# A diffusion trunk layer: modulation vectors by split products, first tiles transposed earlier, the first unit's side steps later

## The chip, the cores and the metric

One core of one Trainium2 chip. The metric is the device time of one execution in microseconds (us), as the median of several executions of the same program. Times inside the program come from one profiled execution and are counted from its first instruction.

## What is computed

One layer of a trunk for 2048 latent tokens and 256 context tokens of width 1024: a bidirectional gated linear recurrence, then a gated feed-forward block. Both are preceded by a normalisation that is shifted and scaled by vectors made from `c` (latent) and `c_ctx` (context). Cut to what this change touches:

```python
sc_lat, sc_ctx = silu(c), silu(c_ctx)
m_l = (sc_lat @ w_ada[l] + b_ada[l])[:, None, :]      # w_ada: 1024 x 6144
m_c = sc_ctx @ w_ada[l] + b_ada[l]
sh1, sc1, g1, sh2, sc2, g2 = split(m_l, 6)
csh1, csc1, ... = split(m_c, 6)
hl = modulate(rmsnorm(lat, norm_g[l, 0]), sh1, sc1)   # h * (1 + scale) + shift
hc = modulate(rmsnorm(cx, norm_g[l, 0]), csh1, csc1)
yc, yl = hgrn2_mixer(hc, hl, hg_w_in[j], ...)          # first step: [hc; hl] @ hg_w_in
lat = lat + g1 * yl
lat = lat + g2 * conv_ffn(modulate(rmsnorm(lat, norm_g[l, 1]), sh2, sc2), ...)
return rmsnorm(lat, final_g)
```

## The kernel before, in words

All data is float32. Large products are done on TensorE (PE) as "split products": a matrix is cut into a high part, rounded by ScalarE (ACT) to the short format fp32r (`split`, L80), and a low part, the rest, which VectorE (DVE) computes by a subtraction (L81). Three fp32r products (high by high, low by high, high by low) then stand for one float32 product (`mm3`, L356 to L358). A product of operands in plain float32 goes through PE as two recorded instructions.

The program opens with the block of L186 to L252. It must produce the first two of the six modulation vectors, shift and scale, for both kinds of token. `w_ada`'s first 2048 columns come in as 16 tiles of 128 x 1024 (512 KB), two for each of eight blocks k of rows. The tile with i = 0 is issued from ACT's queue, that with i = 1 from SyncE's (SP). PE multiplies each as plain float32 with a stationary operand of two columns, silu(c) and silu(c_ctx) (L209), into four accumulators `mps`. ACT copies the four out (L216), 16 small transposes turn them into columns (`mt`, L220), and DVE adds `b_ada` and `norm_g` (L223 to L225): A1 is the scale, B1 the shift.

The tokens are worked in tiles of 128 and units of three tiles (384 columns): the first unit is the two context tiles and one latent tile, the second unit the next three latent tiles. The first three tiles are fetched between the `w_ada` tiles and normalised (`early_x`: ACT takes the sum of squares at L100, GpSimd (POOL) the power at L77, DVE scales at L105). Once A1 and B1 are there, each tile is transposed by PE in two groups of four blocks (`transpose_mod`, L112), modulated out of the accumulator by ACT (L116) or DVE (L119), and split into parts `hh` and `hl` (`put_split`). Then come four more tiles (`early_x(3)` to `early_x(6)`), needed from the second unit on.

The weights of head 0 (`load_feat`, `load_vg`: five tiles of `w_in`, 512 KB each) use the same 13 buffers as the `w_ada` tiles and are split too.

After that, `mixer_scan` runs eight heads by units through `unit` (L383 on). A unit begins with the two gates: two `mm3` of 24 products with 384 columns each, followed by a sigmoid on ACT (L402) and an affine step on DVE (L404). Between the products, `tick` calls side steps from the list `todo`, so that the PE never lacks work: in the first unit of all these are the six `put` steps that transpose, modulate and split the second unit's tiles. `ticks[1]` is the number of product triples over which the list is spread: 20 for a unit with context tiles (L393).

The order of instructions on each engine is not the order of the code: a scheduler of the framework sets it when the program is built, from the dependences and its own idea of durations. Each engine then works strictly through its own row, and a DMA waits for its turn in the row of the engine that issues it.

Of the kernel before, what the change touches and what calls it, by code (L numbers as in the profile page):

```python
# [9 lines left out]
F32 = mybir.dt.float32  # L10
F32R = mybir.dt.float32r
# [3 lines left out]
OP = mybir.AluOpType  # L15
# [4 lines left out]
D = 1024  # L20
# [3 lines left out]
KT = 8  # L24
# [24 lines left out]
def body(ctx, tc, a, out):  # L49
    nc = tc.nc  # L50
    pe, act, dve, pool, sp = nc.tensor, nc.scalar, nc.vector, nc.gpsimd, nc.sync
# [11 lines left out]
    ident = cst.tile([128, 128], F32, name="ident")  # L63
# [15 lines left out]
    def split(h, l, src):  # L79
        act.activation(h, src, AF.Copy)  # L80
        dve.tensor_tensor(l, src, h.bitcast(F32), OP.subtract)  # L81
# [4 lines left out]
    A1 = [small(f"A1_{i}") for i in range(2)]  # L86
    B1 = [small(f"B1_{i}") for i in range(2)]
# [16 lines left out]
        else:  # L104
            dve.tensor_scalar(xt, xt, rs, None, OP.mult)  # L105

    def transpose_mod(xt, hm, g, psp, A, B, tag, bufs, on_act):

        tp = psp.tile([128, 4, 128], F32, name="tp", tag=tag, bufs=bufs)
        for j in range(4):  # L110
            k = g * 4 + j
            pe.transpose(tp[:, j, :], xt[:, k * 128:(k + 1) * 128], ident)  # L112
        for j in range(4):
            k = g * 4 + j
            if on_act:
                act.activation(hm[:, k, :], tp[:, j, :], AF.Identity, bias=B[:, k:k + 1],  # L116
                               scale=A[:, k:k + 1])
            else:
                dve.tensor_scalar(hm[:, k, :], tp[:, j, :], A[:, k:k + 1], B[:, k:k + 1],  # L119
                                  OP.mult, OP.add)  # L120

    ch = ctx.enter_context(ExitStack())
    rawp = pool_(ch, "rawp", 2)
# [5 lines left out]
    late = Sf[:, 0:4]  # L129
# [35 lines left out]
    def load_feat(h, **kw):  # L165


        feat = []
        for ty in (2, 1):
            wh = wp.tile([128, KT, 128], F32R, name="wh", tag="wh")  # L170
            wl = wp.tile([128, KT, 128], F32R, name="wl", tag="wl")
            load_w(h, ty, wh, wl, **kw)
            feat.append((wh, wl))
        vh = wp.tile([128, KT, 384], F32R, name="vh", tag="vh", bufs=1)
        vl = wp.tile([128, KT, 384], F32R, name="vl", tag="vl", bufs=1)
        load_w(h, 0, vh[:, :, 256:], vl[:, :, 256:], **kw)
        return feat, vh, vl
# [8 lines left out]
    with ExitStack() as c0:  # L186
        p0 = pool_(c0, "p0", side="right")
        p0s = pool_(c0, "p0s", space=PSUM)
        act.activation(sil, vec[:, V_C:V_C + 16], AF.Sigmoid)
        dve.tensor_tensor(sil, sil, vec[:, V_C:V_C + 16], OP.mult)  # L190
        silv = sil.rearrange("p (two k) -> p k two", two=2)
        mps = [p0s.tile([2, 512], F32, name=f"mps{n}") for n in range(4)]
        staged = [v[:, i] for p, n in ((2, 3), (5, 3), (4, 1))
                  for v in [place(p, [128, n, D], F32, "x0")] for i in range(n)]

        def early_x(j):

            xt = x_tile(None, first[j], xt=staged[j])
            junk = p0.tile([128, D], F32, name="junk", tag="hm", bufs=3)
            normalize(xt, junk, p0)  # L200

        first = [t for u in GROUPS[0] for t in u]
        for k in range(KT):
            for i in range(2):
                wt = p0.tile([128, D], F32, name="wada", tag="wada", bufs=13)
                (sp if i else act).dma_start(
                    wt, a["w_ada"][k * 128:(k + 1) * 128, i * D:(i + 1) * D])
                for n in range(2):
                    pe.matmul(mps[2 * i + n], silv[:, k, :], wt[:, n * 512:(n + 1) * 512],  # L209
                              start=k == 0, stop=k == KT - 1)  # L210
            if 3 <= k < 6:
                early_x(k - 3)
        head0 = load_feat(0, p=p0, tag="wada", bufs=13)
        m2 = [rawp.tile([2, 2, 512], F32, name="m2", tag="raw") for _ in range(2)]
        for n in range(4):
            ada_done = act.activation(m2[n // 2][:, n % 2], mps[n], AF.Copy)  # L216
        m2f = [m.rearrange("p a b -> p (a b)") for m in m2]
        mt = p0s.tile([128, 16, 2], F32, name="mt")
        for j in range(16):
            pe.transpose(mt[:, j, :], m2f[j // 8][:, j % 8 * 128:(j % 8 + 1) * 128],  # L220
                         ident[0:2, 0:2])
        for i in (1, 0):
            dve.tensor_tensor(B1[i], mt[:, 0:8, i], vec[:, V_BA:V_BA + 8], OP.add)  # L223
            dve.tensor_tensor(A1[i], mt[:, 8:16, i], vec[:, V_BA + 8:V_BA + 16], OP.add)
            dve.scalar_tensor_tensor(A1[i], A1[i], 1.0, vec[:, V_NG:V_NG + 8], OP.add, OP.mult)  # L225
        hms = [p0.tile([128, KT, 128], F32, name="hm", tag="hm", bufs=3) for _ in range(3)]
        for g in range(2):
            ks = slice(g * 4, g * 4 + 4)
            for j, hm in enumerate(hms):
                m = 0 if first[j] >= 0 else 1  # L230
                transpose_mod(staged[j], hm, g, p0s, A1[m], B1[m], "tr", 3, (g + j) % 2)
                put_split(hm, 0, j, ks)
        with tc.issue_after(ada_done.ins):
            load_vg(0, head0, p=p0, tag="wada", bufs=13)
        for j in range(3, 7):
            early_x(j)


        l0, l1 = vec[:, V_LB:V_LB + 16], vec[:, V_LB + 16:V_LB + 32]
        mx = p0.tile([128, 16], F32, name="mx")  # L240
        e2 = p0.tile([128, 2, 16], F32, name="e2")
        eb = p0.tile([128, 32], F32, name="eb")
        pool.memset(eb, float(np.e))
        dve.tensor_tensor(mx, l0, l1, OP.max)
        dve.tensor_tensor(e2[:, 0], l0, mx, OP.subtract)
        dve.tensor_tensor(e2[:, 1], l1, mx, OP.subtract)
        e2f = e2.rearrange("p a b -> p (a b)")
        pool.tensor_tensor(e2f, eb, e2f, OP.pow)
        dve.tensor_tensor(mx, e2[:, 0], e2[:, 1], OP.add)
        dve.reciprocal(mx, mx)  # L250
        dve.tensor_tensor(lb, e2[:, 0], mx, OP.mult)
        dve.tensor_tensor(oml, e2[:, 1], mx, OP.mult)  # L252
# [26 lines left out]
    def mixer_scan():  # L279
# [82 lines left out]
        def unit(h, w, u, tiles, todo, fine=False):  # L362
# [4 lines left out]
            s0 = sum(t < 0 for t in tiles)  # L367
# [22 lines left out]

            done = [0]

            ticks = [0, 20 if s0 else 42]  # L393
            if not fine:
                tick = None

# [1 line left out]
            for d in range(2):  # L398
# [4 lines left out]
                j = (1 - d) * NH + h  # L403
# [3 lines left out]
            v = gp.tile([128, NSC, 128], F32, name="v", tag="v", bufs=2)  # L407
# [241 lines left out]
        g1s = []  # L649
        rest = ada_rest()  # L650
        todo = [f for j in range(3, 6) for f in make_h(1, j - 3, first[j], staged[j])]
        steps, fine = 0, True
        third = [make_h(2, i, t, None if i else staged[6]) for i, t in enumerate(GROUPS[0][2])]
        new = [make_h(u, i, t) for u, tiles in enumerate(GROUPS[1]) for i, t in enumerate(tiles)]
        for g, units in enumerate(GROUPS):
            for h in range(NH):
# [5 lines left out]
                for u, tiles in enumerate(units):  # L662
                    todo, fine = list(unit(h, w, u, tiles, todo, fine)), False
# [722 lines left out]
    for i, (j, cs) in enumerate(pieces):  # L1386
# [9 lines left out]
        if cs.start:  # L1396
            v = V[:, j]
# [31 lines left out]
```

## Time and profile before

| | |
|---|---|
| median of the runs before | 2866.76 us |
| lowest of the runs before | 2860.11 us |
| the profiled execution | 2865.12 us |
| its span, first to last instruction | 2863.1 us |
| PE busy in the span | 2805.9 us (98%) |
| mean granted TensorE clock | 0.994 of full speed |

How to read it: the profile lists what each engine did and what ended each idle time before an instruction. A line of the timeline gives the start and the length in us, the engine, the line of the kernel, the operation, the tile written and the tiles read, the shape, a count where equal instructions follow each other, and in brackets the idle time before it with the one that released it. Recorded lengths of instructions that follow each other on one engine overlap a little, so the price of one in a row is the distance from start to start. The granted clock is 1.00 at TensorE's upper level (2.4 GHz) and 0.50 at the lower (1.2 GHz).

### The profile page before, as it was taken

How to read it: one execution, taken by the hardware profiler on the slowest of the kernel's cores; microseconds unless marked ns; L12 is line 12 of the kernel's file. 1: busy time of each engine (PE TensorE's matmuls, PEld its weight loads, DVE VectorE, ACT ScalarE, POOL GpSimd, SP SyncE). 2: the span in 40 equal slices, each digit the busy share in tenths (PEclk: the TensorE clock that was granted, in tenths of full speed). 3: DMA queues.
4: the chain of work that ended last, by engine and by line, in shares of the span. 5: the costliest groups of instructions: out<-in, count | busy, mean ns of one | idle time of the engine just before them, and what ended most of it. 6: DMA issues, size and time to landing. Idle time of an engine off the chain costs nothing.

```text
span 2863.1 us, 43709 instructions
## 1 busy us (share of the span) xinstructions
PE 2805.9 (98%) x16016; PEld 2506.1 (88%) x16016; DVE 2110.5 (74%) x3690; ACT 1174.4 (41%) x2515; POOL 594.3 (21%) x1028
## 2 busy tenths in 40 slices
PE   7999999999999999998999799999999999999999
PEld 4999999999999999997888688888888888887887
DVE  5766666677666666577987698887888887677887
ACT  5433333365333333333555444444444444333343
POOL 2111111121111111111111353343444432000001
PEclk9999999999999999999999899999999999999999
DMA  6222222222222222135677622225522224887663
GB/s 236 69 80 77 84 79 78 78 86 81 85 90 71 84 69 87 62 94 183 266 290 276 257 88 89 82 81 176 206 88 71 77 89 136 284 298 251 196 203 122
DMA packets 202911, 386.56 MB, mean 135 GB/s; under 512 B 26692, under 2 KB 117828, under 8 KB 197448
## 3 DMA queue, kind: packets, MB, share of 16 engines
q1 hardware_dynamic: 199960, 375.51, 39.1%
q10 hardware_dynamic: 2736, 8.26, 0.8%
q8 instruction: 126, 2.06, 0.3%
q14 instruction: 89, 0.73, 0.1%
HBM read 281.70 MB, written 101.99 MB: 134 GB/s over the span
## 4 chain that ended last, share of the span: by engine, by line
PE 89%; DVE 4%; DMA 3%; ACT 2%; issue 1%; POOL 1%; SPq 0%; DVEq 0%; ACTq 0%; POOLq 0%
PE z L358 10%; PE z L356 10%; PE z L357 10%; PE y L1263 4%; PE y L1262 4%; PE y L1261 4%; PE zc L741 3%; PE zd L741 3%; PE zd L738 3%; PE zc L738 3%; PE zc L740 3%; PE zd L740 3%; PE za L741 3%; PE za L738 3%; PE za L740 3%; PE kv L574 2%
## 5 line engine op out<-in xcount | busy, mean ns | idle before, releaser
L356 PE MATMUL z<-vh,hh 128*128 128x256 f32 (+1 forms) x1024 | 300.3, 293 | 0.0
L358 PE MATMUL z<-vh,hl 128*128 128x256 f32 (+1 forms) x1024 | 293.5, 287 | 0.0
L357 PE MATMUL z<-vl,hh 128*128 128x256 f32 (+1 forms) x1024 | 293.3, 286 | 0.0
L356 PE MATMUL z<-hh,wh 128*128 128x384 f32 x768 | 264.0, 344 | 0.7 <-ACT hh L80 0.7
L357 PE MATMUL z<-hl,wh 128*128 128x384 f32 x768 | 258.5, 337 | 0.5 <-DVE hl L81 0.5
L358 PE MATMUL z<-hh,wl 128*128 128x384 f32 x768 | 258.7, 337 | 0.0
L1263 PE MATMUL y<-wd,ml 128*128 128x512 f32 x600 | 234.0, 390 | 2.3 <-DVE ml L81 2.1
L1261 PE MATMUL y<-wd,mh 128*128 128x512 f32 x600 | 233.8, 390 | 0.7 <-DVE P L1315 0.6
L1262 PE MATMUL y<-wd,mh 128*128 128x512 f32 x600 | 233.4, 389 | 0.0
L356 PEld LDWEIGHTS z<-vh,hh 128*128 128x128 f32 x1024 | 196.3, 192 | 0.0
L357 PEld LDWEIGHTS z<-vl,hh 128*128 128x128 f32 x1024 | 196.1, 191 | 0.0
L358 PEld LDWEIGHTS z<-vh,hl 128*128 128x128 f32 x1024 | 195.7, 191 | 0.0
L81 DVE TENSOR_TENSOR w<-s,w 128x512 fp32r<-128x512 f32 x132 | 145.1, 1106 | 61.6 <-ACT w L80 61.6
L484 POOL COPY TX<-S 128x3 f32<-128x3 f32 x48 | 14.6, 305 | 791.9 <-DVE S L448 791.9
L80 ACT ACTIVATE w<-raw 128x512 fp32r<-128x512 f32 x176 | 109.1, 628 | 111.6 <-DMA raw<-in_w_up_dram 43.9
L424 DVE TENSOR_TENSOR st<-z,st 128x128 f32<-128x128 f32 x127 | 36.6, 289 | 158.4 <-ACT st L423 158.2
L81 DVE TENSOR_TENSOR w<-raw,w 128x512 fp32r<-128x512 f32 x176 | 122.9, 701 | 40.4 <-ACT w L80 40.0
L1025 DVE SCALAR_TENSOR_TENSOR r<-uv,conv,r 128x1023 f32<-128x1023 f32 (+1 forms) x88 | 149.5, 1716 | 0.4
L356 PEld LDWEIGHTS z<-hh,wh 128*128 128x128 f32 x768 | 145.3, 189 | 4.4 <-DVE acc L620 1.7
L419 ACT ACTIVATE v<-z 128x128 f32<-128x128 f32 x128 | 35.5, 278 | 271.1 <-PE z L358 271.0
L357 PEld LDWEIGHTS z<-hl,wh 128*128 128x128 f32 x768 | 145.1, 189 | 0.7 <-DVE hl L81 0.7
L358 PEld LDWEIGHTS z<-hh,wl 128*128 128x128 f32 x768 | 144.8, 188 | 0.0
(325 smaller groups left out, 8172.9 us busy)
## 6 DMA issues: line engine op xcount, KB each, us to landing
raw<-in_w_up_dram SPq DMA_DIRECT2D x90, 512.0 KB, 3.9
raw<-in_w_in_dram SPq DMA_DIRECT2D x80, 512.0 KB, 3.7
lr<-m SPq DMA_DIRECT2D x49, 512.0 KB, 5.6
m<-r SPq DMA_DIRECT2D x66, 256.0 KB, 4.7
raw<-in_w_ada_dram SPq DMA_DIRECT2D x32, 512.0 KB, 4.4
stash<-st SPq DMA_DIRECT2D x125, 128.0 KB, 1.9
kq<-stash SPq DMA_DIRECT2D x15, 1024.0 KB, 7.3
og<-stash SPq DMA_DIRECT2D x15, 1024.0 KB, 6.4
```

The lines of the kernel that those rows point to most:

```text
L80: act.activation(h, src, AF.Copy)
L81: dve.tensor_tensor(l, src, h.bitcast(F32), OP.subtract)
L356: pe.matmul(o, sh[:, k], mh[:, k], start=k == 0, stop=False)
L357: pe.matmul(o, sh[:, k], ml[:, k], start=False, stop=False)
L358: pe.matmul(o, sl[:, k], mh[:, k], start=False, stop=k == KT - 1)
L738: pe.matmul(o, w[:, 0, k], r[:, :, 0, k], start=start and k == 0, stop=False, skip_group_check=True)
L740: pe.matmul(o, w[:, 0, k], r[:, :, 1, k], start=False, stop=False, skip_group_check=True)
L741: pe.matmul(o, w[:, 1, k], r[:, :, 0, k], start=False, stop=k == 3, skip_group_check=True)
L1025: dve.scalar_tensor_tensor(r, x, cw, r, OP.mult, OP.add)
L1261: pe.matmul(z, lh, rh, start=start, stop=False, skip_group_check=True)
L1262: pe.matmul(z, lh, rl, start=False, stop=False, skip_group_check=True)
L1263: pe.matmul(z, ll, rh, start=False, stop=stop, skip_group_check=True)
```

## The change

Three things, all in the opening and the first unit:

- The `w_ada` tiles are split by ACT and DVE like all other large operands, and so is the stationary operand: `s4` holds the high parts of silu(c) and silu(c_ctx) in two columns and the low parts in two more. Each tile then takes four fp32r products (high and low part, two halves of 512 columns) in place of two float32 ones. The accumulators have four rows; after the small transposes two DVE steps add the low columns to the high ones.
- The first group of transposes of the first three tiles is written ahead of the end of the `w_ada` loop (`transpose4`), and the modulation of the result stays behind it (`modulate`).
- In the first unit `ticks` starts at -8: no side step is called before the first gate's eight triples are through; the six are then spread over 20 ticks.

```diff
+        s4 = p0.tile([128, KT, 4], F32R, name="s4")
+        split(s4[:, :, 0:2], s4[:, :, 2:4], silv)
+        mps = [p0s.tile([4, 512], F32, name=f"mps{n}") for n in range(4)]
...
                 (sp if i else act).dma_start(
                     wt, a["w_ada"][k * 128:(k + 1) * 128, i * D:(i + 1) * D])
-                for n in range(2):
-                    pe.matmul(mps[2 * i + n], silv[:, k, :], wt[:, n * 512:(n + 1) * 512],
-                              start=k == 0, stop=k == KT - 1)
+                wh = rawp.tile([128, D], F32R, name="wh", tag="raw")
+                wl = p0.tile([128, D], F32R, name="wl", tag="wal", bufs=2)
+                split(wh, wl, wt)
+                for v in (wh, wl):
+                    for n in range(2):
+                        pe.matmul(mps[2 * i + n], s4[:, k], v[:, n * 512:(n + 1) * 512],
+                                  start=k == 0 and v is wh, stop=k == KT - 1 and v is wl)
             if 3 <= k < 6:
                 early_x(k - 3)
+            if k >= KT - 2:
+                for j in ((0, 1), (2,))[k - KT + 2]:
+                    tps[0, j] = transpose4(staged[j], 0, p0s, "tr", 3)
...
+        dve.tensor_copy(ml, mt4[:, :, 2:4])
+        dve.tensor_tensor(mt, mt4[:, :, 0:2], ml, OP.add)
...
-                transpose_mod(staged[j], hm, g, p0s, A1[m], B1[m], "tr", 3, (g + j) % 2)
+                if g:
+                    tps[g, j] = transpose4(staged[j], g, p0s, "tr", 3)
+                modulate(tps[g, j], hm, g, A1[m], B1[m], (g + j) % 2)
...
-            ticks = [0, 20 if s0 else 42]
+            late_ = fine == "late"
+            ticks = [-8, 20] if late_ else [0, 20 if s0 else 42]
...
-        steps, fine = 0, True
+        steps, fine = 0, "late"
```

The scheduler also moves what the diff does not name. The row of SP at the program's start, before (`x_140` and `x_143` are the first three tiles, `x_141`/`x_142` and `x_144`/`x_145` the next four, `raw` the weights of head 0):

```order
L206 DMA wada<-in_w_ada_dram 128x1024 x2
L152 DMA x_140<-in_ctx_dram 128x1024
L206 DMA wada<-in_w_ada_dram 128x1024 x2
L152 DMA x_140<-in_ctx_dram 128x1024
L206 DMA wada<-in_w_ada_dram 128x1024 x2
L152 DMA x_140<-in_x_dram 128x1024
L206 DMA wada<-in_w_ada_dram 128x1024 x2
L162 DMA raw<-in_w_in_dram 128x1024 x5
L152 DMA x_141<-in_x_dram 128x1024 x3
L152 DMA x_142<-in_x_dram 128x1024
```

The same stretch of SP's row in the changed kernel:

```order
L218 DMA wada<-in_w_ada_dram 128x1024 x2
L160 DMA x_143<-in_ctx_dram 128x1024 x2
L218 DMA wada<-in_w_ada_dram 128x1024 x2
L160 DMA x_143<-in_x_dram 128x1024
L160 DMA x_144<-in_x_dram 128x1024 x2
L218 DMA wada<-in_w_ada_dram 128x1024
L160 DMA x_144<-in_x_dram 128x1024
L160 DMA x_145<-in_x_dram 128x1024
L218 DMA wada<-in_w_ada_dram 128x1024 x3
L170 DMA raw<-in_w_in_dram 128x1024 x7
```

The four later tiles have moved from behind the weights of head 0 to a place ahead of the last three or four `w_ada` tiles of SP's row.

ACT's row where the modulation vectors are finished, before (`wh` and `vh` from `raw` are high parts of head 0's weights, `m` the copies of the accumulators, `hm` a modulated block):

```order
L100 ACTIVATE junk,ss<-x_140 128x1024
L80 ACTIVATE wh<-raw 128x1024 x2
L80 ACTIVATE vh<-raw 128x8x128
L216 ACTIVATE m_249<-mps_136 2x512
L216 ACTIVATE m_249<-mps_137 2x512
L216 ACTIVATE m_250<-mps_138 2x512
L216 ACTIVATE m_250<-mps_139 2x512
L80 ACTIVATE vh<-raw 128x8x128
L116 ACTIVATE hm<-tp,B_1_108,A_1_106 128x128 x4
```

ACT's row at the same place in the changed kernel:

```order
L80 ACTIVATE wh<-wada 128x1024 x2
L218 DMA wada<-in_w_ada_dram 128x1024
L80 ACTIVATE wh<-wada 128x1024 x3
L80 ACTIVATE wh<-raw 128x1024
L80 ACTIVATE wh<-wada 128x1024
L80 ACTIVATE wh<-raw 128x1024
L236 ACTIVATE m_363<-mps_139 4x512
L80 ACTIVATE vh<-raw 128x8x128
L236 ACTIVATE m_363<-mps_140 4x512
L236 ACTIVATE m_364<-mps_141 4x512
L236 ACTIVATE m_364<-mps_142 4x512
L80 ACTIVATE vh<-raw 128x8x128 x2
```

ACT issues its last `w_ada` tile behind the splits of the pair k = 5, and between the split of that tile and the first modulation (the row that follows, `hm` x4) stand six other splits of 128x1024 and the four copies.

DVE's row where the second unit's tiles are normalised, before (`x_141`, `x_142`: the four later tiles; `hm`: the first modulated group of the second unit; `F_430`: the first gate):

```order
L76 TENSOR_SCALAR rs<-ss 128x1 x2
L105 TENSOR_SCALAR x_141<-x_141,rs 128x1024 x2
L76 TENSOR_SCALAR rs<-ss 128x1
L105 TENSOR_SCALAR x_141<-x_141,rs 128x1024
L76 TENSOR_SCALAR rs<-ss 128x1
L105 TENSOR_SCALAR x_142<-x_142,rs 128x1024
L119 TENSOR_SCALAR hm<-tp,A_0_105,B_0_107 128x128 x4
L404 TENSOR_SCALAR F_430<-F_430,oml,lb 128x12x32
```

The same stretch of DVE's row in the changed kernel:

```order
L105 TENSOR_SCALAR x_144<-x_144,rs 128x1024
L76 TENSOR_SCALAR rs<-ss 128x1
L105 TENSOR_SCALAR x_144<-x_144,rs 128x1024
L76 TENSOR_SCALAR rs<-ss 128x1
L105 TENSOR_SCALAR x_144<-x_144,rs 128x1024
L76 TENSOR_SCALAR rs<-ss 128x1
L105 TENSOR_SCALAR x_145<-x_145,rs 128x1024
L432 TENSOR_SCALAR F_533<-F_533,oml,lb 128x12x32
L127 TENSOR_SCALAR hm<-tp,A_0_105,B_0_107 128x128 x4
```

The first gate's affine step now stands ahead of the second unit's first modulation, and both still stand behind all four normalisations. From the second unit's fifth group of transposes on (L112 before, at 80.55 us of the profile) the rows of all five engines are the same in both kernels, names apart.

## Rows read from the trace of the kernel before

**Rows 1.** The page's head: span, then busy time and instructions of each engine.

```profile
span 2863.1 us, 43709 instructions
PE 2805.9 (98%) x16016; PEld 2506.1 (88%) x16016; DVE 2110.5 (74%) x3690; ACT 1174.4 (41%) x2515; POOL 594.3 (21%) x1028
```

**Rows 2.** The page's chain that ended last: shares of the span by engine.

```profile
PE 89%; DVE 4%; DMA 3%; ACT 2%; issue 1%; POOL 1%; SPq 0%; DVEq 0%; ACTq 0%; POOLq 0%
```

**Rows 3.** Windows: us, busy PE, PEld, DVE, ACT, POOL, granted clock, DMA share, GB/s.

```profile
10.00:20.00 10.00, 10.00 (x25) 1.98 (x24) 3.90 (x9) 2.30 (x4) 7.00 (x26) 1.00 1.03 410
...
48.00:49.00 1.00, 0.00 (x0) 0.00 (x0) 0.35 (x2) 0.92 (x1) 0.86 (x2) 0.50 0.00 0
...
55.00:56.00 1.00, 1.00 (x8) 0.97 (x8) 0.89 (x2) 0.56 (x2) 0.00 (x0) 1.00 0.02 8
```

**Rows 4.** PE's timeline from 0 to 81 us.

```profile
4.89 30.11 PE L209 MATMUL mps<-wada,sil 128*2 128x512 f32 x64 [4.89 <-DVE sil L190]
...
44.09 0.33 PE L357 MATMUL z<-hl,wh 128*128 128x384 f32 x1
44.26 0.34 PE L358 MATMUL z<-hh,wl 128*128 128x384 f32 x1
49.53 1.11 PE L112 MATMUL tp<-ident,x 128*128 128x128 f32 x4 [4.93 <-DVE x L105]
...
53.64 0.52 PE L357 MATMUL z<-hl,wh 128*128 128x384 f32 x1
53.96 0.49 PE L358 MATMUL z<-hh,wl 128*128 128x384 f32 x1
...
65.22 0.66 PE L112 MATMUL tp<-ident,x 128*128 128x128 f32 x4 [1.00 <-ACT hm L116]
...
70.31 0.33 PE L434 MATMUL qz<-ident,qt 128*128 128x128 f32 x1 [1.12 <-ACT hm L116]
...
80.55 0.60 PE L112 MATMUL tp<-ident,x 128*128 128x128 f32 x4
```

**Rows 5.** ACT's timeline from 29 to 55 us.

```profile
29.39 1.06 ACT L80 ACTIVATE wh<-raw 128x1024 fp32r<-128x1024 f32 x1 [3.59 <-DMA raw<-in_w_in_dram]
...
31.95 1.06 ACT L80 ACTIVATE vh<-raw 128x1024 fp32r<-128x1024 f32 x1 [0.23 <-DMA raw<-in_w_in_dram]
32.91 1.05 ACT L216 ACTIVATE m<-mps 2x512 f32<-2x512 f32 x2
...
37.46 1.51 ACT L116 ACTIVATE hm<-tp,B,A 128x128 f32<-128x128 f32 x4 [0.89 <-DVE A L224]
38.85 1.07 ACT L80 ACTIVATE vh<-raw 128x1024 fp32r<-128x1024 f32 x1
...
46.19 0.67 ACT L80 ACTIVATE hh<-hm 128x512 fp32r<-128x512 f32 x1
...
48.08 1.06 ACT L100 ACTIVATE junk<-x 128x1024 f32<-128x1024 f32 x1 [0.19 <-ACT junk L100]
...
54.55 0.49 ACT L402 ACTIVATE F<-z 128x384 f32<-128x384 f32 x1 [4.27 <-PE z L358]
```

**Rows 6.** DVE's timeline from 30 to 55 us.

```profile
30.48 2.50 DVE L81 TENSOR_TENSOR wl<-raw,wh 128x1024 fp32r<-128x1024 f32 x2 [3.03 <-ACT wh L80]
...
47.25 0.69 DVE L81 TENSOR_TENSOR hl<-hm,hh 128x512 fp32r<-128x512 f32 x1
...
52.62 0.76 DVE L105 TENSOR_SCALAR x<-x,rs 128x1024 f32<-128x1024 f32 x1 [0.71 <-POOL rs L77]
53.29 1.37 DVE L119 TENSOR_SCALAR hm<-tp,A,B 128x128 f32<-128x128 f32 x4
```

**Rows 7.** DMA issues from 0 to 60 us: count, KB each, median us to landing.

```profile
wada<-in_w_ada_dram ACTq DMA_DIRECT2D x8, 512.0 KB, 7.2
wada<-in_w_ada_dram SPq DMA_DIRECT2D x8, 512.0 KB, 9.8
```

**Rows 8.** The page's costliest groups: mean ns of one product of 512 columns in fp32r.

```profile
L1262 PE MATMUL y<-wd,mh 128*128 128x512 f32 x600 | 233.4, 389 | 0.0
```

More of the change, by code (lines that the diff above doesn't have):

```diff
@@ L105, in normalize, with transpose4 @@
             dve.tensor_scalar(xt, xt, rs, None, OP.mult)
-    def transpose_mod(xt, hm, g, psp, A, B, tag, bufs, on_act):
+    def transpose4(xt, g, psp, tag, bufs):
         tp = psp.tile([128, 4, 128], F32, name="tp", tag=tag, bufs=bufs)
@@ L112, in transpose_mod, with modulate @@
             pe.transpose(tp[:, j, :], xt[:, k * 128:(k + 1) * 128], ident)
+        return tp
+    def transpose_mod(xt, hm, g, psp, A, B, tag, bufs, on_act):
+        modulate(transpose4(xt, g, psp, tag, bufs), hm, g, A, B, on_act)
+    def modulate(tp, hm, g, A, B, on_act):
         for j in range(4):
@@ L191, in body @@
         silv = sil.rearrange("p (two k) -> p k two", two=2)
-        mps = [p0s.tile([2, 512], F32, name=f"mps{n}") for n in range(4)]
+        s4 = p0.tile([128, KT, 4], F32R, name="s4")
+        split(s4[:, :, 0:2], s4[:, :, 2:4], silv)
+        mps = [p0s.tile([4, 512], F32, name=f"mps{n}") for n in range(4)]
+        tps = {}
         staged = [v[:, i] for p, n in ((2, 3), (5, 3), (4, 1))
@@ L207, in body @@
                     wt, a["w_ada"][k * 128:(k + 1) * 128, i * D:(i + 1) * D])
-                for n in range(2):
-                    pe.matmul(mps[2 * i + n], silv[:, k, :], wt[:, n * 512:(n + 1) * 512],
-                              start=k == 0, stop=k == KT - 1)
+                wh = rawp.tile([128, D], F32R, name="wh", tag="raw")
[5 more added lines that the diff above has]
+                                  start=k == 0 and v is wh, stop=k == KT - 1 and v is wl)
             if 3 <= k < 6:
                 early_x(k - 3)
+            if k >= KT - 2:
+                for j in ((0, 1), (2,))[k - KT + 2]:
+                    tps[0, j] = transpose4(staged[j], 0, p0s, "tr", 3)
         head0 = load_feat(0, p=p0, tag="wada", bufs=13)
-        m2 = [rawp.tile([2, 2, 512], F32, name="m2", tag="raw") for _ in range(2)]
+        m2 = [rawp.tile([4, 2, 512], F32, name="m2", tag="raw") for _ in range(2)]
         for n in range(4):
@@ L217, in body @@
         m2f = [m.rearrange("p a b -> p (a b)") for m in m2]
-        mt = p0s.tile([128, 16, 2], F32, name="mt")
+        mt4 = p0s.tile([128, 16, 4], F32, name="mt4")
         for j in range(16):
-            pe.transpose(mt[:, j, :], m2f[j // 8][:, j % 8 * 128:(j % 8 + 1) * 128],
-                         ident[0:2, 0:2])
+            pe.transpose(mt4[:, j, :], m2f[j // 8][:, j % 8 * 128:(j % 8 + 1) * 128],
+                         ident[0:4, 0:4])
+        mt = p0.tile([128, 16, 2], F32, name="mt")
+        ml = p0.tile([128, 16, 2], F32, name="ml")
+        dve.tensor_copy(ml, mt4[:, :, 2:4])
+        dve.tensor_tensor(mt, mt4[:, :, 0:2], ml, OP.add)
         for i in (1, 0):
```

## The prediction, made before the changed kernel ran

> **What bounds the kernel now.** I read the page's head first, then the chain, then the windows and timelines of the opening, where all the edits lie. PE is busy for 2805.9 of 2863.1 us [rows 1] and is 89% of the chain [rows 2]: whatever moves the start of PE's unbroken row moves the end by as much. So the whole question is when PE reaches the point from which both programs are the same. I call it P; it is the group of transposes at 80.55 us [rows 4].
>
> Up to P the reader is to see four stretches. (a) From 4.89 us to 35.00 us PE works on the float32 products, 64 records in 30.11 us, 0.94 us for each of the 32 products [rows 4]; this, and not the transfers, ends the stage. (b) Meanwhile the transfers run at their limit: 410 GB/s [rows 3], and two tiles of 512 KB that follow each other land 2.56 us after a third (29.39 to 31.95 on ACT [rows 5]), 1.28 us each. (c) At 37.46 ACT starts to modulate; the last high part of the first unit is split at 46.19 [rows 5], the last low part ends at 47.25 + 0.69 = 47.94 [rows 6]. (d) PE begins the first gate, stops after 12 products at 44.6 and idles 4.93 us, since a side step's tile is not normalised yet [rows 4]. In that idle time the clock falls to 0.50 [rows 3]; the next products stand 0.32 us apart (53.64 to 53.96) against 0.17 (44.09 to 44.26) [rows 4]. The first gate is through at 54.55, when its sigmoid starts [rows 5].
>
> The profiled execution took 2865.12 us, 2.0 more than its span; the median of the runs is 2866.76, 1.6 above it. I add to the profiled execution.
>
> **The products.** The 32 float32 products go, 30.1 us of PE. In come 64 fp32r products of 512 columns. A product with four stationary columns is not in the trace; the nearest are 0.39 us as one's recorded length [rows 8] above and the distance of 0.17 us for 384 columns [rows 4] below: 64 x 0.39 = 25 us or 64 x 0.17 = 11 us, both under the 29 us that this stage's 23 tiles need at 1.28 us. Either way PE no longer ends it. ACT gains 16 splits of 128x1024 at 0.96 (31.95 to 32.91 [rows 5]), 15 us, and DVE 16 at 1.25 (2.50 for two [rows 6]), 20 us; both fit beside the transfers too, tile by tile 1.25 against 1.28. What is left of them lies behind the last tile to land. The small splits of the stationary operand, the two extra DVE steps and the taller accumulators I cost at nothing: they lie under the splits that ACT does at that moment, and would cost below 1 us together.
>
> **The transfers.** Before, head 0's first weight tile lands at 29.39 [rows 5] as the 20th of the 512 KB tiles. In the new row of SP four tiles of x come ahead of the last `w_ada` tiles, so the last of 23 tiles before the weights lands no earlier than 29.39 + 3 x 1.28 = 33.2. The second brake is ACT's row: it issues its last `w_ada` tile only once it reaches the splits of pair k = 5, whose later tile is the 19th in order and lands near 28.1; ACT's tiles took 7.2 us to land, SP's 9.8 [rows 7], so this one lands near 35.3 or, at SP's pace, 37.9. Bounds 33.2 and 37.9; I take 35.0, next to ACT's own row.
>
> The Trainium skill speaks against the change here: "DMA: Bandwidth & Descriptors", section "Issuing engines are not separate DMA queues", says that loads started by different engines run on the same 16 DMA engines and interleave, so a second issuing engine saves only the time of issuing. By that rule alone the four x tiles hold back the last `w_ada` tile to 33.2 whichever engine issues it, and the sum below would be 1.8 us smaller. The row on landing times (7.2 against 9.8) agrees that both queues share one limit, but shows that they are not served evenly.
>
> **From the last tile to the first modulation.** In ACT's new row there follow seven splits of 128x1024 (two of `w_ada`, five weights of head 0 between them) and four copies at 0.53 (two in 1.05 [rows 5]): 7 x 0.96 + 4 x 0.53 = 8.8 us. The first modulation starts at 43.8 instead of 37.46. The transposes of group 0 written ahead take nothing from this: they were PE's, and PE was not what ACT waited for.
>
> **From there to the first gate.** Before, ACT needed 46.19 + 0.67 - 37.46 = 9.4 us for modulations, high parts, one sum of squares and one weight split of 0.96 [rows 5]; that split is now done earlier, and ACT waits a little for PE's second groups: 8.9, so the last high part is ready at 52.7. The last low part ended 47.94 - 46.86 = 1.1 later before; now 53.8. About 11 products of the first gate are then left, at 0.17: through at 55.7, against 54.55. So 6 us of lateness shrink to 1.1, since the 4.93 us wait and the slow products after it are no longer in the way.
>
> **After the first gate.** What did not wait before now does. The four normalisations that ran during PE's idle time stand on ACT and DVE between the first unit's last split and the first gate's steps: about 1.2 us each there (a sum of squares is 1.06 [rows 5], a DVE pass is 0.76 with 0.71 of waiting for POOL [rows 6]), so they end at 58.7; then the gate's affine step, 0.5, and the second unit's first modulation, 1.37 [rows 6]: 60.5. The next group of transposes waits for that, for there is one accumulator tile for them. PE has one group and 16 products to do meanwhile, 0.4 + 2.8 from 55.7 on, and waits from 58.9 to 60.5: 1.6 us. The waits of 1.00 and 1.12 [rows 4] I leave as they are. PE's other work between the gate and P is the same but for one more group of transposes (+0.4) and three products done ahead (-0.5).
>
> P moves by 1.1 + 1.6 = 2.7 us, to 83.2. Behind P nothing differs, and PE carries the shift to the end: 2865.1 + 2.7 = **2867.8 us**. With the landing at 33.2 it is +0.9, at 37.9 it is +5.6: 2866.0 to 2870.7.
>
> **The rivals.**
> - Not slower (0.22). The last `w_ada` tile lands at 33.2 and the 1.6 us wait hides, because POOL and DVE turn the normalisations round faster than I count. Then 2.7 - 1.8 - 1.6 = -0.7: 2864.4. For it speaks that all x tiles have landed early; against it, that by this count ACT's row has hardly a gap from 35 to 57.
> - Slower through the clock (0.15). PE has next to nothing between the small transposes near 42 and the gate near 49. Before, 4.93 us of idleness brought it to the lower level, with products 0.15 us dearer [rows 4]. If the idle times around 53.8 keep it there for the rest of the first gate and all of the second, 11 + 24 products cost 5.2 more: 2873.0. It decides from the point where those products come in two bursts with ACT's splits between them. The Trainium skill, "TensorE: Matmul & The Clock Gate", section "HAM oscillation — how this bites in real kernels", describes this: bursts with waits for data between them run cold each time. The trace agrees for one such wait, and shows none in a row.
> - The change does not shorten what it means to (part of the forecast): the products get cheap, but the vectors come later.
>
> **How the numbers follow.** Forecast 0.61 (2866.0 to 2870.7), not slower 0.22, clock 0.15, 0.02 for what I don't see. The runs shown lie down to 2860.1, 5 us below the profiled one, so the low end is 2864.4 - 5 = 2859; the high end takes in the clock's 2873 and a little: 2874. What a measurement of this kernel can tell from no change is about 2%, 57 us, more than the opening's whole 45 us up to the first gate's stop; no case reaches it: faster 0.01, same 0.98, slower 0.01.
>
> **What would show it.** Right: the first modulation near 43.8; no wait of 4.9 us before the first gate's end; the first gate's sigmoid at 56 to 57; a wait of 1 to 2 us before the second unit's second group of transposes; P near 83. The transfers step falls if the last `w_ada` split starts before 33; the ACT step if the first modulation starts below 41; the last step if PE has no wait between 56 and 62. The whole is wrong if P lies below 80.

## The result, and the profile after

The changed kernel takes 2871.72 us (median of 20 runs) against 2865.51 us before (20 runs; the 2866.76 us further up is the median of the first three): a ratio of 1.0024 with an interval of 1.0017 to 1.0031, or 4.9 to 8.9 us more. It is slower, as forecast, and inside the outer range of 2859 to 2874 us, but not inside the forecast's own 2866.0 to 2870.7: the shift is 6.2 us by the medians and 6.9 by the ratio, where 2.7 were worked out and 5.6 was the upper bound. The profiled execution took 2870.17 us.

The head of its page and its chain, to be held against [rows 1] and [rows 2]:

```profile
span 2868.5 us, 43768 instructions
PE 2804.0 (98%) x16016; PEld 2510.2 (88%) x16016; DVE 2126.9 (74%) x3709; ACT 1187.9 (41%) x2532; POOL 590.6 (21%) x1028
...
PE 86%; DMA 5%; DVE 4%; ACT 2%; POOL 1%; issue 1%; SPq 0%; DVEq 0%; POOLq 0%; ACTq 0%
```

PE has 1.9 us less to do in a span that is 5.4 us longer. The chain gives 3% of the span from PE to others, 2% of it to DMA. Where that is, the windows of the opening show (us, busy PE, PEld, DVE, ACT, POOL, granted clock, DMA share, GB/s):

```profile
20.00:30.00 10.00, 5.83 (x26) 1.67 (x24) 6.12 (x8) 4.53 (x8) 1.08 (x2) 1.00 1.03 411
30.00:40.00 10.00, 7.97 (x21) 1.83 (x22) 6.75 (x6) 7.00 (x8) 0.00 (x0) 0.66 0.88 351
40.00:50.00 10.00, 5.01 (x29) 3.16 (x28) 9.36 (x23) 9.73 (x19) 0.00 (x0) 0.69 0.35 107
50.00:60.00 10.00, 9.54 (x38) 8.70 (x39) 7.65 (x18) 8.14 (x17) 2.16 (x4) 0.63 0.31 105
...
70.00:80.00 10.00, 7.14 (x37) 6.58 (x36) 5.50 (x16) 6.47 (x15) 2.52 (x8) 0.72 0.03 9
```

In the `w_ada` stage, where PE was never free [rows 3], it now works 5.83 us of 10 and the transfers are the limit. From 40 to 50 us ACT and DVE have hardly a gap and PE is half idle. The clock is at its lower level from 31 to 37 us, from 44 to 57 and again from 75 to 81; before, it was low only around 50 behind the first 30 us. ACT's timeline, with the lines that answer to [rows 5]:

```profile
29.98 0.34 ACTq L218 DMA_DIRECT2D wada<-in_w_ada_dram  x1
...
36.88 1.06 ACT L80 ACTIVATE wh<-wada 128x1024 fp32r<-128x1024 f32 x1 [2.44 <-DMA wada<-in_w_ada_dram]
...
40.69 0.57 ACT L236 ACTIVATE m<-mps 4x512 f32<-4x512 f32 x1
...
45.44 1.46 ACT L124 ACTIVATE hm<-tp,B,A 128x128 f32<-128x128 f32 x4
...
59.21 0.49 ACT L430 ACTIVATE F<-z 128x384 f32<-128x384 f32 x1 [1.53 <-PE z L384]
```

The first modulation starts at 45.44 (37.46 before, 8.0 later), the first gate's sigmoid at 59.21 (54.55 before, 4.7 later). PE's timeline, for [rows 4]; its first four lines are products of the `w_ada` stage, at the low and at the full clock:

```profile
34.43 1.91 PE L225 MATMUL mps<-wh,s 128*4 128x512 f32 x4
36.14 0.97 PE L225 MATMUL mps<-wl,s 128*4 128x512 f32 x2
...
38.22 0.62 PE L225 MATMUL mps<-wl,s 128*4 128x512 f32 x2
38.68 0.40 PE L225 MATMUL mps<-wh,s 128*4 128x512 f32 x1
...
46.95 1.97 PE L112 MATMUL tp<-ident,x 128*128 128x128 f32 x8 [2.67 <-ACT hm L124]
...
55.15 0.52 PE L383 MATMUL z<-hl,wh 128*128 128x384 f32 x1
55.47 0.52 PE L384 MATMUL z<-hh,wl 128*128 128x384 f32 x1
...
57.56 0.34 PE L383 MATMUL z<-hl,wh 128*128 128x384 f32 x1
57.74 0.33 PE L384 MATMUL z<-hh,wl 128*128 128x384 f32 x1
...
74.70 0.45 PE L462 MATMUL qz<-ident,qt 128*128 128x128 f32 x1 [2.22 <-DVE hm L127]
...
79.05 0.52 PE L382 MATMUL z<-hh,wh 128*128 128x384 f32 x1
79.37 0.52 PE L383 MATMUL z<-hl,wh 128*128 128x384 f32 x1
...
88.32 0.60 PE L112 MATMUL tp<-ident,x 128*128 128x128 f32 x4
```

The 4.93 us wait before the first gate's end is gone. But PE's first product of that gate starts only at 51.02, most of the gate's products (until 57.4) stand 0.32 us apart, and so do those at 79 us, behind the longer wait at `qz`. P comes at 88.32 instead of 80.55: 7.8 later.

Two measures are used below. The median's interval is 4 us wide or more, and those of the changed kernel, e1 and e4 to e11 overlap, so medians do not tell these runs apart. Part of the spread does not come from the opening: behind 1300 us the traces have stretches of lower clock that are not the same in each (0.93 of full speed from 1600 to 1650 us in the profiled run before, 0.86 in the one after). So beside the median stands the **offset**: how much later than before the sigmoid starts that stands at 231.04 us in the trace before. It stays the same to 0.4 us from there to 1290 us. The row that it is counted from, in ACT's timeline of the kernel before:

```profile
231.04 0.49 ACT L402 ACTIVATE F<-z 128x384 f32<-128x384 f32 x1 [1.32 <-PE z L358]
```

The same sigmoid in ACT's timeline of the changed kernel:

```profile
238.66 0.49 ACT L430 ACTIVATE F<-z 128x384 f32<-128x384 f32 x1 [1.33 <-PE z L384]
```

The offset of the changed kernel is 7.6 us. Each offset is that of one profiled execution; the same rows up to 30 us start 1.1 us later in e1's trace than in the changed kernel's, so differences of 1 us are not read.

### The profile page after: what moved, and what is told of

Its sections match the earlier page's. It is cut to its first block, busy times and chain, and to the rows that moved or that the text cites. A ratio compares the mean times of both kernels' runs of the same rounds, so it can differ in the third digit from the quotient of the medians.

```text
span 2868.5 us, 43768 instructions
## 1 busy us (share of the span) xinstructions
PE 2804.0 (98%) x16016; PEld 2510.2 (88%) x16016; DVE 2126.9 (74%) x3709; ACT 1187.9 (41%) x2532; POOL 590.6 (21%) x1028
## 4 chain that ended last, share of the span: by engine, by line
PE 86%; DMA 5%; DVE 4%; ACT 2%; POOL 1%; issue 1%; SPq 0%; DVEq 0%; POOLq 0%; ACTq 0%
PE z L384 10%; PE z L382 10%; PE z L383 10%; PE y L1291 3%; PE y L1289 3%; PE y L1290 3%; PE zc L769 3%; PE zd L769 3%; PE zc L768 3%; PE zd L768 3%; PE zd L766 3%; PE zc L766 3%; PE za L769 3%; PE za L768 3%; PE za L766 3%; PE kv L602 2%
```

## The experiments

All times are us from the span's start; the last column is the median and the one of the kernel before on the same chip.

| run | first modulation | first sigmoid | third sigmoid | offset | median / before |
|---|---|---|---|---|---|
| before | 37.46 | 54.55 | 75.47 | 0 | 2865.5 |
| changed | 45.44 | 59.21 | 84.51 | +7.6 | 2871.7 / 2865.5 |
| e1 split products alone | 46.46 | 59.48 | 85.28 | +9.2 | 2872.2 / 2864.5 |
| e2 early transposes alone | 38.20 | 54.87 | 75.41 | -0.7 | 2865.2 / 2864.5 |
| e3 late steps alone | 38.00 | 52.09 | 78.63 | +1.6 | 2865.6 / 2864.5 |
| e4 x tiles behind | 44.16 | 56.90 | 82.01 | +5.1 | 2869.2 / 2864.5 |
| e5 idle products | 48.44 | 63.42 | 87.30 | +10.4 | 2875.5 / 2863.7 |
| e6 xt early | 45.71 | 58.54 | 83.62 | +6.7 | 2870.4 / 2863.7 |
| e7 last tiles from SP | 45.44 | 59.74 | 84.53 | +7.7 | 2872.8 / 2863.7 |
| e8 e4 and e7 | 44.14 | 58.24 | 83.04 | +6.2 | 2871.4 / 2863.7 |
| e9 idle products, other bank | 45.83 | 57.80 | 83.57 | +6.7 | 2870.4 / 2863.7 |
| e10 value weights behind | 45.06 | 60.46 | 86.42 | +9.3 | 2871.2 / 2863.7 |
| e11 e4 and e10 | 42.31 | 57.70 | 83.63 | +6.8 | 2871.6 / 2863.7 |
| e12 no passes of ACT over w_ada | 35.50 | 49.02 | 75.55 | -1.5 | 2862.7 / 2864.2 |

**The parts, each alone.**

e1, the changed kernel with the other two parts undone:

```diff
-            if k >= KT - 2:
-                for j in ((0, 1), (2,))[k - KT + 2]:
-                    tps[0, j] = transpose4(staged[j], 0, p0s, "tr", 3)
...
-        steps, fine = 0, "late"
+        steps, fine = 0, True
```

> The split products alone: the steps of the first unit keep their old ticks and no tile is transposed ahead of the end of w_ada. The four x tiles of the second unit and the seventh tile (2 MB) stand ahead of the last w_ada tiles in SP's queue, as in the changed kernel. Theory A (the cost sits at the end of the w_ada stage: transfers ahead of its last tiles, splits in ACT's row, then a slow clock): 5 to 9 us above the kernel before, first gate's sigmoid at 58 to 60 us. Rival B (the new place of the first unit's steps costs most): 1 to 4 us above.

Ratio 1.0027 (1.0017 to 1.0036), offset 9.2, sigmoid at 59.48: theory A. The split products alone cost what the whole change costs; the other two parts take back 1.6 at most in their company, of which 1.1 lie in the stage's later start in this trace. By the medians and their intervals the two cannot be told apart.

e2, the kernel before with the `transpose4`/`modulate` lines alone.

> The early transposes alone, products in fp32 with two stationary columns as before. Theory A: within 1 us of the kernel before, last wait for the first high part no shorter, since ACT and DVE are busy there. Rival C (transposes in the stream of fp32 products push the end of the stage): 1 to 3 us above.

Ratio 0.9998 (0.9990 to 1.0007), offset -0.7: no effect that can be told. The first modulation waits for DVE's `A` there, not for transposes.

e3, the kernel before with `ticks = [-8, 20]` in the first unit.

> The later ticks alone: everything of the opening as before. Theory A: within 1.5 us of the kernel before, or up to 2 us below, since the 4.9 us wait of TensorE at 44 to 49 us, which ends with a normalised tile of the second unit, goes. Rival B: 3 to 5 us above, as the second unit's steps then come too late.

Ratio 1.0006 (0.9997 to 1.0015), offset +1.6: theory A by the median, at its upper edge by the offset, and no gain. The first gate is 2.5 us earlier, and all of it is lost by the third gate, which is 3.2 us later. PE's timeline shows where, before and behind the gate:

```profile
47.44 0.44 PE L356 MATMUL z<-hh,wh 128*128 128x384 f32 x1 [2.29 <-ACT hh L80]
...
56.62 0.66 PE L112 MATMUL tp<-ident,x 128*128 128x128 f32 x4 [1.40 <-DVE hm L119]
...
67.25 0.66 PE L112 MATMUL tp<-ident,x 128*128 128x128 f32 x4 [2.15 <-ACT hm L116]
```

The 4.93 us wait of [rows 4] is not slack that this order of the steps cashes in: ACT and DVE work on the second unit's tiles in that time, and without the wait PE waits for them further on. Another order was not tried.

**The transfers.** e4, in the changed kernel, the four later x tiles queued on SP behind the first five head weights:

```diff
-        for j in range(3, 7):
-            early_x(j)
+        with tc.issue_after(w_in_dma[-1]):
+            for j in range(3, 7):
+                early_x(j)
```

> The changed kernel with the four x tiles that are needed later queued behind the first five head weights on SP. Theory A, its transfer step: 2 MB at 410 GB/s are 5.1 us, so the last w_ada tile lands at about 32 us, the first modulation starts at 40 to 42 us and the time is 3 to 5 us under the changed kernel, 2 to 4 us above the kernel before. Rival D (ACT's splits and not the transfers set the first modulation): it starts at 44 us or later, and the time is within 1.5 us of the changed kernel, 5.5 to 8 us above the kernel before.

Ratio 1.0013 (1.0004 to 1.0022), offset 5.1, between the two: a gain of 2.5 us by the offset and 1.5 by the medians. The first modulation, at 44.16, is the rival's, so theory A's mechanism is not what gained it. ACT's timeline:

```profile
28.77 0.33 ACTq L220 DMA_DIRECT2D wada<-in_w_ada_dram  x1
...
35.61 1.06 ACT L80 ACTIVATE wh<-wada 128x1024 fp32r<-128x1024 f32 x1 [2.10 <-DMA wada<-in_w_ada_dram]
```

The tile that ACT issues last is split 1.3 us earlier, not 5: it is still issued from ACT's row at 28.77, behind a split, and lands 6.8 us after its issue as before. The rest of the gain lies between the modulation and the first sigmoid (12.7 us instead of 13.8); what makes it was not tried. So ACT's late issue seemed the brake; e7 issues the last two tiles of the first half from SP:

```diff
-                (sp if i else act).dma_start(
+                (sp if i or k >= KT - 2 else act).dma_start(
```

> The changed kernel with the last two w_ada tiles of the first half issued from SP too, so that their issue does not stand behind a split in ACT's row. Theory (the last tile is late because ACT issues it late): its split starts 2 to 3 us earlier than 36.9 us, ACT's 2.4 us idle before it goes, the first modulation starts at about 43 us, 2 to 3 us under the changed kernel. Rival (the transfers are the limit, whoever issues them): within 1 us of it.

Offset 7.7, ratio 1.0029 (1.0020 to 1.0039): no gain, the rival's number but not its reason. ACT's timeline:

```profile
32.69 2.19 ACT L80 ACTIVATE wh<-wada 128x1024 fp32r<-128x1024 f32 x2 [0.39 <-PE mps L225]
35.93 2.04 ACT L80 ACTIVATE wh<-wada 128x1024 fp32r<-128x1024 f32 x2 [1.04 <-PE mps L225]
38.73 1.06 ACT L236 ACTIVATE m<-mps 4x512 f32<-4x512 f32 x2 [0.77 <-PE mps L225]
...
42.60 2.93 ACT L80 ACTIVATE vh<-raw 128x1024 fp32r<-128x1024 f32 x3
45.44 1.46 ACT L124 ACTIVATE hm<-tp,B,A 128x128 f32<-128x128 f32 x4
```

The 2.44 us of waiting for the transfer are gone, and the first modulation starts at 45.44 all the same. SP issues its last `w_ada` tile at 23.3 us, where ACT issued its own at 29.98. ACT now waits for PE to free the two buffers of high parts, copies the accumulators out earlier, and has the head's splits behind instead of between. PE is the brake here: the chain that ended last runs through its products from 31.41 us for 4.5 us, and the granted clock is 0.50 from 30 to 34 us in this trace. What the low clock costs in the `w_ada` stage was not tried; in the changed kernel these products are not on the chain.

e8 does both.

> Both edits of the transfer queue: the four later x tiles behind the first five head weights, and the last two w_ada tiles of the first half from SP. Theory: 10 MB at 410 GB/s, so the last w_ada tile is there at 28 to 30 us, the first modulation starts at 39 to 41 us, 4 to 6 us under the changed kernel, 1 to 3 us above the kernel before. Rival (ACT's splits bound the end of the stage): the first modulation not before 43 us, 1.5 to 3 us under the changed kernel.

First modulation 44.14: the rival. Its time is 1.4 us under the changed kernel by the offset (6.2), just short of the rival's 1.5, and not under it by the median (ratio 1.0027, 1.0017 to 1.0038). With the tiles there in time, the 32 passes over `w_ada`, waits of 0.4 to 0.7 us for PE's products and the five splits of the head's weights are what is left ahead of the modulation.

**The row of ACT.** e10 moves the three value-weight splits from ahead of the first modulation to behind the first unit:

```diff
+        with tc.issue_after(last_hi[0].ins):
+            load_w(0, 0, head0[1][:, :, 256:], head0[2][:, :, 256:], p=p0, tag="wada", bufs=13)
             load_vg(0, head0, p=p0, tag="wada", bufs=13)
```

> The changed kernel with the three value-weight splits of head 0 (vh, vl) moved in ACT's and VectorE's rows from ahead of the first modulation to behind the last split of the first unit; PE's row and the transfers as they are. ACT-row theory: the three cost 2.85 us of ACT there and VectorE's A comes earlier too, so the first modulation starts at 43.0 to 44.3 us instead of 45.4, the first gate's sigmoid 1.2 to 2.5 us earlier, and the offset to the kernel before at 230 us into the span falls from 7.6 to 5 to 6.5 us. Rival (the splits only move: the second unit's squares and products then wait): sigmoid earlier, but the offset within 1 us of 7.6.

Offset 9.3, ratio 1.0029 (1.0018 to 1.0040): worse than either theory. ACT's timeline:

```profile
45.06 1.51 ACT L126 ACTIVATE hm<-tp,B,A 128x128 f32<-128x128 f32 x4 [1.46 <-DVE A L252]
...
53.96 2.95 ACT L82 ACTIVATE vh<-raw 128x1024 fp32r<-128x1024 f32 x3
...
59.40 1.06 ACT L102 ACTIVATE junk<-x 128x1024 f32<-128x1024 f32 x1 [0.41 <-DVE rs L76]
60.46 0.47 ACT L434 ACTIVATE F<-z 128x384 f32<-128x384 f32 x1
```

The modulation gains 0.4 us, since DVE's `A` is late too. The three splits then stand ahead of the second unit's sums of squares, and the first sigmoid stands behind those in ACT's row. e11 adds e4's edit:

> Both: the four later x tiles behind the head weights in SP's queue (as in e4) and the value-weight splits behind the first unit. If the two steps add up: first modulation at 42 to 43 us, offset at 230 us of 3 to 4.5 us above the kernel before, where e4 has 5.1. If one hides the other: offset of 5 us or more.

First modulation at 42.31 as expected, offset 6.8 and not 3 to 4.5; ratio 1.0028 (1.0017 to 1.0039): one hides the other. The earlier modulation, bought with work put behind it, is given back here.

**The clock.** e5 puts 22 idle products (nothing reads their results) of 448 columns into PE's gaps; they write unused columns of the bank of `mt4`.

> The changed kernel with 22 idle products (4 x 448 columns, into columns of the modulation's bank that nothing reads) in TensorE's gaps between the last w_ada product and the first unit's products. Clock theory: the granted clock stays at 1.00 from 44 to 57 us, the first products come 0.17 and not 0.32 us apart, the first gate's sigmoid starts 1 to 2 us earlier (57.2 to 58.2 us), since the last low part comes at 55.4 us whatever the clock, and the time is 1 to 2 us under the changed kernel. Rival (the clock is the larger half of the miss): 3 to 4 us under it. Rival (the gate waits for the last low part alone): no change.

This one missed. The clock does hold while they run (1.00 from 42 to 48 us), but the first modulation is 3 us later. ACT's timeline:

```profile
48.44 1.51 ACT L126 ACTIVATE hm<-tp,B,A 128x128 f32<-128x128 f32 x4 [2.31 <-DVE A L261]
```

Since the idle products write the tile that DVE reads the vectors from, DVE waits for the last of them. The run says nothing of the clock. e9 has 13 of them, into the first `w_ada` bank, which is copied out by then:

```diff
+            with tc.issue_after(ins):
+                for _ in range(n):
+                    pe.matmul(mps[0][:, 0:448], s4[:, 0], wz, start=True, stop=True)
```

> The clock again: 13 idle products (4 x 448 columns) in TensorE's gaps between 44 and 52 us, now into a bank of the w_ada products that is already copied out, so that the modulation vectors don't wait for them as they did in e5. Clock theory: the first modulation still starts at 45.4 us, the granted clock stays at 1.00 to 57 us, the first gate's sigmoid starts 1 to 2 us earlier than 59.2 us, and the time is 1 to 2 us under the changed kernel (5.5 to 6.5 us above the kernel before at 230 us into the span, where it is 7.6 us now). Rival (only the last low part counts): sigmoid at 59 us or later, no change.

Ratio 1.0018 (1.0009 to 1.0027). The window of the first gate (columns as in the windows above):

```profile
46.00:60.00 14.00, 12.06 (x61) 9.09 (x60) 11.78 (x29) 12.17 (x27) 2.63 (x4) 0.91 0.35 118
```

PE's timeline at the end of that gate and behind it:

```profile
54.71 0.62 PE L394 MATMUL z<-hh,wh 128*128 128x384 f32 x2 [0.20 <-ACT hh L80]
55.52 0.44 PE L395 MATMUL z<-hl,wh 128*128 128x384 f32 x1 [0.19 <-DVE hl L81]
55.80 0.34 PE L396 MATMUL z<-hh,wl 128*128 128x384 f32 x1
55.98 0.34 PE L394 MATMUL z<-hh,wh 128*128 128x384 f32 x1
...
62.46 0.65 PE L114 MATMUL tp<-ident,x 128*128 128x128 f32 x4 [1.36 <-DVE hm L129]
...
74.78 0.30 PE L474 MATMUL qz<-ident,qt 128*128 128x128 f32 x1 [1.97 <-DVE hm L129]
```

With the clock at 0.91 over 46 to 60 us (0.59 in the changed kernel) the products are 0.17 to 0.18 apart, wait for the last parts, and the sigmoid starts at 57.80, 12.0 us behind the first modulation instead of 13.8. But e6 below, with the order of the changed kernel and no idle products, needs 12.8 (its clock is at 0.65 over the same stretch). So the low clock costs the first gate 0.9 to 1.8 us in these traces. Behind the gate nothing of it can be read: PE waits 1.36 us at 62.46 where it had no wait, `qz` comes when it came, the offset of 6.7 is 0.9 under the changed kernel's and the same as e6's, and the median shows no gain. The clock is a consequence of the waits here and a small part of the cost.

**The late xt tiles.** In the changed kernel the third unit's two tiles are issued at 53.90 (37.31 before), in part because their memory overlaps a buffer that a head weight still uses. e6 has one more `w_ada` buffer and the low parts in a pool of their own; every engine's row is unchanged, and the two tiles are issued at 44.82.

> The changed kernel with the same order on every engine, but one more w_ada buffer and the low parts of w_ada in a pool of their own, so that the third unit's two x tiles (xt) take memory that is free early and don't wait for the split of a head weight. Theory (the late xt tiles hold GpSimd's and VectorE's rows, qz waits 2.2 us at 74.7 us and the clock falls again): xt lands before 50 us, qz's wait falls to about 1.1 us, the slow stretch at 75 to 81 us goes, 2 to 3 us under the changed kernel. Rival (qz waits for the high and low parts in any case): within 1 us of the changed kernel.

Offset 6.7, ratio 1.0024 (1.0015 to 1.0033): the rival's number. The wait at `qz` is 2.22 us as in the changed kernel, on the same DVE step; early xt tiles are worth 1 us at most while the rows stay as they are.

**The passes themselves.** e12 leaves out the low part of `w_ada`, and DVE makes the high copies:

```diff
-                split(wh, wl, wt)
-                for v in (wh, wl):
-                    for n in range(2):
-                        pe.matmul(mps[2 * i + n], s4[:, k], v[:, n * 512:(n + 1) * 512],
-                                  start=k == 0 and v is wh, stop=k == KT - 1 and v is wl)
+                dve.tensor_copy(wh, wt)
+                for n in range(2):
+                    pe.matmul(mps[2 * i + n], s4[:, k], wh[:, n * 512:(n + 1) * 512],
+                              start=k == 0, stop=k == KT - 1)
```

> The changed kernel without the low parts of w_ada: VectorE makes one high copy of each w_ada tile, ACT touches none of them, and TensorE does 32 products with four stationary columns instead of 64 (so the low part of w_ada is left out of the modulation). ACT then issues its w_ada tiles unhindered and the later x tiles fall behind the head weights by themselves. Theory (ACT's and VectorE's 32 passes over w_ada are what the change costs, by late issues and by pushing the head weights' splits behind them): the first modulation starts at 36 us or earlier, not at 45.4, the first gate's sigmoid before 53 us, and the offset to the kernel before at 230 us into the span is between -4 and +1.5 us instead of +7.6. Rival (the later steps of the first unit and the slow clock cost as much as the passes): offset +3 us or more.

Offset -1.5, ratio 0.9998 (0.9989 to 1.0007). ACT's timeline:

```profile
29.70 1.06 ACT L234 ACTIVATE m<-mps 4x512 f32<-4x512 f32 x2 [3.96 <-PE mps L223]
...
35.50 1.50 ACT L124 ACTIVATE hm<-tp,B,A 128x128 f32<-128x128 f32 x4
```

PE's timeline behind the first gate:

```profile
54.54 0.66 PE L112 MATMUL tp<-ident,x 128*128 128x128 f32 x4 [2.67 <-DVE hm L127]
```

Without ACT in the stage all its `w_ada` tiles are issued by 18.8 us, the scheduler leaves the x tiles behind the head weights, and the accumulators are copied out at 29.70 instead of 40.69. The first modulation comes 9.9 us earlier than in the changed kernel and the offset falls by 9.1. The theory stands: the passes over `w_ada`, and what they push back, are the cost. The run takes several things away at once (ACT's passes, the low parts with half of the products, and by that the new order of the transfers), so it does not share the cost out; e4, e7 and e8, which change the transfers alone, recover 2.5 us of it at most. And even here, with products at half the old price or less, the first gate's gain of 5.5 us over the kernel before shrinks to 1.5, at waits like the 2.67 us one. No run was measurably faster than the kernel before; this one, which leaves work out, is level with it.

## Why the prediction was right, and where its sizes were wrong

- **Direction, and PE no longer the limit of the stage: right.** PE's 30 us of products go and the time rises, because the vectors come later.
- **The forecast of 2866.0 to 2870.7: missed by 1.0; the outer range held.** The 2871.72 us lie between the forecast and the 2873.0 of the rival on the clock, which had 0.15. Part of that is luck. "PE carries the shift to the end" would make P's 7.8 us 2872.9. In the profiled runs the end moved by 5.4 us: the same rows of ACT are 7.5 us apart at 1300 us, 6.4 at 1600 and 5.4 at 2840, and no run shows why.
- **The last tile's landing, "I take 35.0": 1.9 too early.** Its split starts at 36.88, 6.9 us behind its issue at 29.98. The time to land was nearly right (7.2), but the issue came 1.9 us later than the 28.1 counted: it stands behind a split that itself waited for a tile issued from ACT's row (at 22.92, there at 29.75). The bounds of 33.2 and 37.9 held. The rule weighed there, that a second issuing engine saves only the time of issuing (the Trainium skill, "DMA: Bandwidth & Descriptors", "Issuing engines are not separate DMA queues"), is not decided by e7. The move to the other queue saved 6.7 us of issuing there (23.3 instead of 29.98), and the offset stayed (7.7 against 7.6) with PE as the brake that the chain shows in place of the transfer.
- **From the last tile to the modulation, 8.8 us: measured 8.6.** From there to the last high part 8.9: measured 9.1. ACT's row was read rightly.
- **"About 11 products of the first gate are then left, at 0.17": failed.** The last low part came at 55.4, the sigmoid at 59.21, 3.8 us later and not 1.9. Fifteen products stood between them, the first six 0.32 apart and the rest 0.17. In e9, at the full clock, the step takes 2.3 us (55.46 to 57.80), so about 1.5 of the 1.9 are the clock and 0.4 the count of products; in e6 it takes 3.1. That is the rival on the clock in part: it had the second gate at the low level too, which ran at the full one.
- **"So 6 us of lateness shrink to 1.1, since the 4.93 us wait and the slow products after it are no longer in the way": the step that failed in kind.** 8.0 us shrink to 4.7 at the first sigmoid and are 9.0 again at the third. In e3, which takes this wait away alone, the first gate's 2.5 us are lost again too. The table shows it in every run but e2: the offset is 1.5 to 4.3 us more than the lateness of the first sigmoid, and it stays within 2 us of that of the first modulation. From the third sigmoid on the difference is settled (its lateness is 1.4 to 1.6 us more than the offset in all runs with the late steps, 0.6 in e1 and e2). What the first gate gains is given back between the two.
- **"The waits of 1.00 and 1.12 I leave as they are", and 1.6 us before the second transposes: the place was wrong.** The normalisations took 1.53 us each and not 1.2 (DVE's start at 55.30, 56.82, 58.36 and 59.89), so the second unit's first modulation was done at 62.3 and not 60.5. PE, 3.5 us late out of the first gate, did not wait for it. In its stead `qz` waits 2.22 us and the clock falls again. From the first sigmoid to P it took 29.1 us against 27.5 counted.

Together: 1.9 for the landing, 1.9 for the gate, -0.3 for the rest of ACT's and DVE's row, 1.6 behind the gate are the 5.1 us by which P is later than the 83.2 predicted.

What stays open is how much of the wait at `qz` can be had back. The profile's chain goes over POOL and DVE there. Two lines of POOL's timeline in the changed kernel:

```profile
69.83 0.54 POOL L77 TENSOR_TENSOR rs<-rs,mhalf 128x1 f32<-128x1 f32 x1
...
70.67 0.53 POOL L77 TENSOR_TENSOR rs<-rs,mhalf 128x1 f32<-128x1 f32 x1
```

Two lines of DVE's:

```profile
71.57 0.96 DVE L520 TENSOR_TENSOR kd<-ke,TB 128x768 f32<-128x768 f32 x1 [1.71 <-POOL TB L510]
...
73.19 1.36 DVE L127 TENSOR_SCALAR hm<-tp,A,B 128x128 f32<-128x128 f32 x4
```

DVE's `kd` waits 1.71 us for POOL's `TB`, and behind `kd` in DVE's row stands the modulation that `qz` waits for. Between POOL's steps of `TB` stand two powers, for the third unit's tiles; before, both stood ahead of `TB`, and `kd` waited 0.83 us. e6 brought the tiles earlier but left this order, and `kd` waits 1.73 us there. No run moved the powers, and DVE's row, which is full from 60 to 70 us (9.70 us of 10), was not thinned alone.

## What to carry to other kernels

Before work is taken off the busiest engine in a stage, look at what its neighbours get: here 32 passes on ACT and DVE replaced products that took only PE's time, and five splits of the head's weights (4.8 us), most of which used to fit beside them, came to stand between the last tile and the next stage. An idle time of the bound engine can be gained only if the engines that it waits for have room; test that by taking the wait away alone, as e3 does. And follow a shift past the first step at which it shrinks: what counts is the point behind which the rows are the same.

## What the runs showed of the hardware

- A product of 512 columns with four stationary columns is recorded with 0.39 to 0.40 us, like one with a full operand [rows 8]. In the first lines of the changed kernel's PE timeline above, four of them take 1.71 us from start to start at the low clock (granted 0.50 from 34 to 36 us) and two take 0.46 at the full one (1.00 from 38 to 39 us): 0.43 and 0.23 us each. The prediction's bounds of 0.17 and 0.39 held at the full clock only.
- DVE rounds a 128x1024 tile to fp32r in 0.70 us. ACT takes 0.95 for it (37.84 to 38.79 in the changed kernel, from start to start), and DVE's subtraction of two such tiles 1.14 (39.11 to 40.25 there). e12's DVE timeline, with three roundings in 2.10 us:

```profile
24.14 2.10 DVE L221 CAST wh<-wada 128x1024 fp32r<-128x1024 f32 x3
```

- Where a tile lies decides when its load can start: by e6's edit, which changes no row, two loads are issued at 44.82 instead of 53.90 us.
